# A hybrid decoder trunk on one core: where the second inverse root stands at a change of sub-layer

## The chip, the cores and the metric

One core of a Trainium2 chip runs the whole computation in one launch. The metric is the device time of a run in microseconds (us). The names of the engines are those of the profile: PE is TensorE, DVE is VectorE, ACT is ScalarE, POOL is GpSimd, and SP issues transfers.

## The reference

The input is a residual stream `x` of 512 tokens by 1024 channels in float32. Two layers follow one another, and each layer has four sub-layers. Each sub-layer reads `x` through an RMS norm, and its output goes through a second RMS norm before it is added to `x`:

```python
def rmsnorm(x, g):
    y = x * rsqrt(mean(x * x, axis=-1, keepdims=True) + EPS)
    return y * g

for i in range(DEPTH):                                    # DEPTH = 2
    h = rmsnorm(x, g_ffn1_pre[i])                         # 1: ffn1
    x = x + 0.5 * rmsnorm(swiglu(h, w1_gate[i], w1_up[i], w1_down[i]), g_ffn1_post[i])
    h = rmsnorm(x, g_mix_pre[i])                          # 2: mixer
    ... three head groups read h @ w_in[i]: stick-breaking attention, latent attention, gated convolution
    x = x + rmsnorm(concat(y_sb, y_mla, y_cv) @ w_out[i], g_mix_post[i])
    h = rmsnorm(x, g_ffn2_pre[i])                         # 3: ffn2
    x = x + 0.5 * rmsnorm(swiglu(h, w2_gate[i], w2_up[i], w2_down[i]), g_ffn2_post[i])
    h = rmsnorm(x, g_ple_pre[i])                          # 4: ple
    e = sigmoid(h @ w_ple_gate[i]) * (p[i] @ w_ple_proj[i])
    x = x + rmsnorm(e, g_ple_post[i])
```

So a change of sub-layer holds two norms back to back: the norm behind the old sub-layer, the addition to `x`, and the norm ahead of the new one. With two layers of four sub-layers there are seven such changes inside the kernel: ffn1 to mixer, mixer to ffn2, ffn2 to ple, ple to ffn1, and then the first three again in the second layer.

## The kernel before, in words

**Layout.** Channels lie on the 128 partitions and tokens along the free axis, so `x` is eight tiles of 128 by 512, the K slabs 0 to 7. Every float32 operand of a product is split into a rounded high part and a low rest (`xh`, `xl` for the activations, `wh`, `wl` for the weights), and a product of one slab is three matmuls: high by high, low by high, high by low. ACT makes the high part by a cast, DVE or POOL the low part by a subtraction.

**A change of sub-layer.** `finish` ends the old sub-layer. The last output tiles are computed for the first 256 tokens (`ca`) and then for the last 256 (`cb`), and each half has an inverse root of its own, `ra` and `rb_`. For a half, PE sums the squares with a column of ones into a PSUM tile `st` (L389), `Rstd.col` turns `st` into the inverse root `rt` by nine DVE operations on tiles of two columns (all of them L369: `r_v`, `r_y`, four that write `r_q`, `r_z`, `r_w`, `rt`), and `Rstd.row` lets PE transpose `rt` into a row (L402), which ACT copies to `rbs` (L403). Then `update(k, c)` scales `y` by `rbs` (L579, on DVE for the even slabs and on POOL for the odd ones) and adds it to `x` (L583 or L586, DVE).

`Entry` starts the new sub-layer. `half(c)` walks over the eight slabs: update of slab `k`, ACT's high part `xh` (L467), update of slab `k+1`, DVE's low part `xl` (L470), ACT's square of the new `x` (L434), and POOL's sum of the squares (L444). `products` lets PE follow the first half slab by slab for three output tiles (L488, L489 with `xh`; L493 with `xl`, one slab later). Behind slab 5 (`ROW_AT`) it calls `row_b`, so the two transposes of the row for the second half stand at that place in PE's order, and PE waits there until `rt` of the second half is made. Then comes `half(cb)` and the products of the second half (L286 to L288), a fourth output tile over all 512 tokens (`more`), and an inverse root over all four token blocks for the new sub-layer (`r.col`, on tiles of four columns), whose row (again L402) the new sub-layer's evacuations use.

**What sets the order.** Inside a `manual_schedule(engines={...})` block the named engine keeps the written order; everything else is placed by a scheduler when the kernel is built, and each engine then runs its list in order. In `half` DVE's order is the written one. Operations that were written outside of such a block can be placed between those inside it. Before the change `rb_.col()` stands outside, in `finish`, ahead of the construction of `Entry`.

Of the kernel before, what the change touches and what calls it, by code (L numbers as in the profile page):

```python
# [36 lines left out]
ROW_AT = 5  # L37
MORE = 1
LAG = 1
PROJ = 8  # L40
LAST_POOL = (2, 6)
DIRECT = 2
# [66 lines left out]
HALVES = (slice(0, S // 2), slice(S // 2, S))  # L109
# [49 lines left out]
def hybrid_trunk(ctx: ExitStack, tc: tile.TileContext, a: dict, out: bass.AP):  # L159
# [9 lines left out]
    def slot(dt=F32, name="s", tag="s"):  # L169
        return sp.tile([P, S], dt, tag=tag, name=name, bufs=SLOTS[tag])  # L170
# [6 lines left out]
    def bank(name="ps", tag=None):  # L177
        if tag is None:
            tag = dense[0][turn[0] % len(dense[0])]
            turn[0] += 1  # L180
        return ps.tile([P, S], F32, tag=tag, name=name, bufs=BANKS[tag])
# [10 lines left out]
    def f(ap):  # L192
        return ap.bitcast(F32)
# [45 lines left out]
    def gain(l, name, k):  # L239
        c = G_COLS[name] + k  # L240
        return gains[:, l, c:c + 1]
# [132 lines left out]
    class Rstd:  # L374
# [3 lines left out]
        def __init__(self, dim, cols=slice(0, S), tag="v", eps=None, keep=None):  # L378
            self.dim, self.blocks, self.st, self.tag = dim, blocks(cols), None, tag
            self.kw = dict(eps=eps if eps is None else eps[:, cols.start // P:cols.stop // P], keep=keep)  # L380
# [35 lines left out]
    def blocks(cols):  # L416
        return [slice(c, c + P) for c in range(cols.start, cols.stop, P)]
# [32 lines left out]
    class Entry:  # L450

        def __init__(self, l, name, update, row_b, tag):
            self.l, self.name, self.update, self.row_b = l, name, update, row_b
            self.xs = [(slot(F32R, "xh", tag), slot(F32R, "xl", tag)) for _ in range(NK)]
            self.tiles = [slot(name="sq") for _ in range(4)]
            self.sqs = [self.half(HALVES[0])]

        def half(self, c):  # L460
            sq = Squares(c, tiles=self.tiles)
            with tc.manual_schedule(engines={V.engine}):
                self.update(0, c)
                for k in range(NK):
                    g = gain(self.l, self.name, k)
                    h, lo = (t[:, c] for t in self.xs[k])
                    ia = A.activation(out=h, in_=x[k][:, c], func=AF.Copy, scale=g)  # L467
                    if k + 1 < NK:
                        self.update(k + 1, c)
                    iv = V.scalar_tensor_tensor(out=lo, in0=x[k][:, c], scalar=g, in1=f(h), op0=ALU.mult,  # L470
                                                op1=ALU.subtract)
                    sq.add(x[k][:, c])
            sq.fold()
            if c is HALVES[0]:
                self.tail = ia.ins, iv.ins
            return sq

        def products(self, tiles, more=lambda: None):
# [3 lines left out]
            with tc.manual_schedule(engines={T.engine}):  # L482

                for k in range(NK + LAG):
                    kw = dict(skip_group_check=True)
                    if k < NK:
                        for w, o in tiles:
                            T.matmul(o[:, ca], w[k][0], self.xs[k][0][:, ca], start=k == 0, stop=False, **kw)  # L488
                            T.matmul(o[:, ca], w[k][1], self.xs[k][0][:, ca], start=False, stop=False, **kw)  # L489
                    if k >= LAG:  # L490
                        j = k - LAG
                        for w, o in tiles:
# [28 lines left out]
    def finish(ys, sq, last, compute, evac, gcol, nxt, at, xtag="s", eps=None):  # L521
# [18 lines left out]
        ra, rb_ = Rstd(D, ca, eps=eps), Rstd(D, cb, eps=eps)  # L540
# [49 lines left out]
        if nxt is None:  # L590
# [17 lines left out]
                for k in order:  # L608
                    update(k, cb)
            return None  # L610
        rb_.col()
        return Entry(*nxt, update, row_b, xtag)


    def input_forms(l, name, xs, xtag):
# [116 lines left out]
    def ffn(l, idx, state, nxt, xtag="s", early=None):  # L732
# [121 lines left out]
        def evac(m, c, o):  # L854
            V.tensor_scalar(out=ys[m][:, c], in0=o[:, c], scalar1=half[:, l, idx, m:m + 1], scalar2=None, op0=ALU.mult)
            evac.square = o[:, c]

        return finish(ys, sq, last, compute, evac, None, nxt, AT_DOWN, eps=state.eps)

    def trig():  # L860
# [189 lines left out]
    def mixer(l, state, nxt):  # L1050
# [235 lines left out]
        def evac(m, c, o):  # L1286
            V.tensor_tensor(out=ys[m][:, c], in0=o[:, c], in1=ys[m][:, c], op=ALU.add)

        return finish(ys, sq, last, compute, evac, lambda k: gain(l, "mix_post", k), nxt, AT_OUT)

    def ple(l, state, nxt):
# [7 lines left out]
        def project(m):  # L1299
            if m % 4 == 0:  # L1300
                project.w = load_w(a["ple_proj"][l, m // 4], 8, P)
            o = bank()
            product(o, project.w[m % 4 * 2:m % 4 * 2 + 2], pin)
            t = aslot(name="pp")
            copy(E_PROJ, t, o)
            proj.append(t)

        def weights(m, on="vv"):
            return load_w(a["ple_gate"][l, m], NK, P, on)
# [8 lines left out]
        first = [(weights(m, ON_PLE.split()[m]), bank()) for m in range(FIRST)]  # L1318
        state.products(first, lambda: [project(m) for m in range(PROJ)])
        rb = state.row()  # L1320
        for m in range(PROJ, NK):
            project(m)
# [11 lines left out]
        def compute(m, c, tick=lambda: None):  # L1334
            o = bank()
            product(o, w[m], xs, cols=c, tick=tick)
            return o

        return finish(ys, sq, last, compute, evac, lambda k: gain(l, "ple_post", k), nxt, AT_PLE if nxt else AT_END, "m")

    cos = cst.tile([P, S], F32, name="cos")
# [65 lines left out]
```

## Time and profile before

| | |
|---|---|
| median of 3 runs | 2145.63 us (2145.09 to 2147.61) |
| the profiled execution's own time | 2147.86 us |
| its span in the trace | 2146.1 us |
| busy share: PE, DVE, ACT, POOL | 96%, 72%, 52%, 24% |
| mean granted TensorE clock | 0.984 |

The span runs from the first to the last instruction of the program in the trace, and the execution's own time is 1.8 us longer, for what lies around it. The busy shares are averages over stages: in the forty slices of the page PE stands at 90% or more nearly everywhere, and DVE moves between 30% and 90%. The columns of a timeline row are start, duration, engine, line, operation, output and inputs, and in brackets the idle time of the engine before it and what ended that time.

### The profile page before, as it was taken

How to read it: one execution, taken by the hardware profiler on the slowest of the kernel's cores; microseconds unless marked ns; L12 is line 12 of the kernel's file. 1: busy time of each engine (PE TensorE's matmuls, PEld its weight loads, DVE VectorE, ACT ScalarE, POOL GpSimd, SP SyncE). 2: the span in 40 equal slices, each digit the busy share in tenths (PEclk: the TensorE clock that was granted, in tenths of full speed). 3: DMA queues.
4: the chain of work that ended last, by engine and by line, in shares of the span. 5: the costliest groups of instructions: out<-in, count | busy, mean ns of one | idle time of the engine just before them, and what ended most of it. 6: DMA issues, size and time to landing. Idle time of an engine off the chain costs nothing.

```text
span 2146.1 us, 35942 instructions
## 1 busy us (share of the span) xinstructions
PE 2059.6 (96%) x13264; PEld 1874.2 (87%) x13264; DVE 1553.6 (72%) x2851; ACT 1116.6 (52%) x2296; POOL 506.6 (24%) x498
## 2 busy tenths in 40 slices
PE   8999999999989999999989999999999899999996
PEld 6999988887888999888879998888878889998886
DVE  7888754778878788636798786357788798885376
ACT  6556533555656555524565555235455565564243
POOL 3111012126432111003431110031263421100043
PEclk9999999999999999999999999999999999999998
DMA  7777332211133876332427763322111348753321
GB/s 218 172 180 177 89 104 72 91 60 52 55 79 108 196 173 148 100 99 79 122 84 196 178 163 93 98 68 93 53 59 46 88 126 192 180 137 96 98 73 65
DMA packets 139425, 244.73 MB, mean 114 GB/s; under 512 B 15600, under 2 KB 26096, under 8 KB 139248
## 3 DMA queue, kind: packets, MB, share of 16 engines
q1 hardware_dynamic: 117792, 204.00, 30.9%
q0 software_dynamic: 20736, 37.76, 11.2%
q8 instruction: 104, 1.70, 0.3%
q10 hardware_dynamic: 720, 0.67, 0.1%
q14 instruction: 73, 0.60, 0.1%
HBM read 240.27 MB, written 2.10 MB: 113 GB/s over the span
## 4 chain that ended last, share of the span: by engine, by line
PE 82%; DVE 12%; ACT 2%; issue 1%; DMA 1%; POOL 0%; SPq 0%; DVEq 0%; ACTq 0%; POOLq 0%
PE ps L286 9%; PE ps L287 9%; PE ps L288 9%; PE ux L698 6%; PE ux L697 6%; PE ux L696 6%; PE uy L698 3%; PE uy L697 3%; PE uy L696 3%; PE in L286 2%; PE in L287 2%; PE in L288 2%; DVE xl L470 2%; DVE wl L271 2%; PE uz L698 2%; PE uz L697 2%
## 5 line engine op out<-in xcount | busy, mean ns | idle before, releaser
L271 DVE TENSOR_TENSOR wl<-raw,wh 128x512 fp32r<-128x512 f32 (+2 forms) x893 | 605.8, 692 | 393.4 <-ACT wh L270 340.8
L270 ACT CAST wh<-raw 128x512 fp32r<-128x512 f32 (+1 forms) x934 | 548.7, 605 | 577.9 <-PE ps L287 275.1
L444 POOL TENSOR_TENSOR sq<-sq 128x256 f32<-128x256 f32 (+1 forms) x165 | 172.6, 1046 | 730.5 <-ACT sq L434 726.3
L287 PE MATMUL ps<-l,wh 128*128 128x512 f32 (+1 forms) x824 | 302.2, 367 | 0.0
L288 PE MATMUL ps<-h,wl 128*128 128x512 f32 (+1 forms) x824 | 301.8, 367 | 0.4 <-DVE wl L271 0.4
L286 PE MATMUL ps<-h,wh 128*128 128x512 f32 (+1 forms) x824 | 300.2, 368 | 0.0
L680 POOL DMA_DIRECT2D raw<-in_w_gu x144 | 125.9, 915 | 678.0 <-DMA raw<-in_w_gu 181.8
L698 PE MATMUL ux<-fh,wl 128*128 128x256 f32 x864 | 244.5, 283 | 0.0
L697 PE MATMUL ux<-fl,wh 128*128 128x256 f32 x864 | 244.5, 283 | 0.0
L696 PE MATMUL ux<-fh,wh 128*128 128x256 f32 x864 | 244.4, 283 | 0.0
L288 PEld LDWEIGHTS ps<-h,wl 128*128 128x128 f32 x824 | 155.4, 189 | 25.9 <-DVE wl L271 1.3
L287 PEld LDWEIGHTS ps<-l,wh 128*128 128x128 f32 x824 | 155.5, 189 | 24.8 <-DVE l L199 0.2
L286 PEld LDWEIGHTS ps<-h,wh 128*128 128x128 f32 x824 | 155.4, 189 | 24.6
L696 PEld LDWEIGHTS ux<-fh,wh 128*128 128x128 f32 x864 | 165.8, 192 | 0.5
L697 PEld LDWEIGHTS ux<-fl,wh 128*128 128x128 f32 x864 | 165.8, 192 | 0.5
L698 PEld LDWEIGHTS ux<-fh,wl 128*128 128x128 f32 x864 | 165.8, 192 | 0.0
L286 PE MATMUL ps<-xh,wh 128*128 128x512 f32 (+1 forms) x416 | 133.3, 356 | 15.5 <-ACT wh L270 9.8
L287 PE MATMUL ps<-xl,wh 128*128 128x512 f32 (+1 forms) x416 | 142.0, 352 | 1.2 <-DVE xl L470 1.2
L288 PE MATMUL ps<-xh,wl 128*128 128x512 f32 (+1 forms) x416 | 142.2, 350 | 0.0
L286 PEld LDWEIGHTS ps<-xh,wh 128*128 128x128 f32 x416 | 77.4, 196 | 28.7 <-ACT wh L270 11.2
L686 DVE TENSOR_TENSOR raw<-raw 128x512 f32<-128x512 f32 x144 | 98.6, 684 | 0.1
L287 PEld LDWEIGHTS ps<-xl,wh 128*128 128x128 f32 x416 | 80.6, 194 | 10.4 <-DVE xl L470 2.0
(347 smaller groups left out, 5237.1 us busy)
## 6 DMA issues: line engine op xcount, KB each, us to landing
raw<-in_w_gu SPq DMA_DIRECT2D x424, 256.0 KB, 4.0
raw<-in_w_down SPq DMA_DIRECT2D x160, 256.0 KB, 2.7
raw<-in_w_gu POOLq DMA_DIRECT2D x144, 256.0 KB, 5.1
raw<-in_win_f SPq DMA_DIRECT2D x60, 256.0 KB, 2.7
raw<-in_ple_gate SPq DMA_DIRECT2D x32, 256.0 KB, 2.7
raw<-in_wo_a SPq DMA_DIRECT2D x18, 256.0 KB, 2.8
raw<-in_w_down SPq DMA_DIRECT2D x32, 128.0 KB, 2.2
raw<-in_wo_b SPq DMA_DIRECT2D x12, 256.0 KB, 2.7
```

What stands on the lines that cost most here:

```text
L270: A.copy(out=h, in_=raw)
L271: (G if on == "g" else V).tensor_tensor(out=lo, in0=raw, in1=f(h), op=ALU.subtract)
L286: T.matmul(oc, wh, xh[:, cols], start=first and k == 0, stop=False, **kw)
L287: T.matmul(oc, wh, xl[:, cols], start=False, stop=False, **kw)
L288: product.last = T.matmul(oc, wl, xh[:, cols], start=False, stop=last and k == n - 1, **kw)
L444: G.tensor_tensor(out=self.acc[:, c], in0=self.acc[:, c], in1=self.last[:, c], op=ALU.add)
L470: iv = V.scalar_tensor_tensor(out=lo, in0=x[k][:, c], scalar=g, in1=f(h), op0=ALU.mult, op1=ALU.subtract)
L680: G.dma_start(out=self.raw[n], in_=self.part(m), accum_op=ALU.add)
L686: V.tensor_tensor(out=r, in0=r, in1=self.raw[p], op=ALU.add)
L696: T.matmul(o, wh, xh, start=first and k == 0, stop=False, **kw)
L697: T.matmul(o, wh, xl, start=False, stop=False, **kw)
L698: T.matmul(o, wl, xh, start=False, stop=k == 3, **kw)
```

## The change

`rb_.col`, the nine operations that make the second half's `rt`, is handed to `Entry` as a function, and `half` calls it in the first half's walk, directly behind the low part of slab 4 (the fifth slab). It now stands inside the block that keeps DVE's written order. What is computed is the same, and each operation is there as often as before.

```diff
 ROW_AT = 5
 MORE = 1
 LAG = 1
+COL_AT = 4
...
-        def __init__(self, l, name, update, row_b, tag):
-            self.l, self.name, self.update, self.row_b = l, name, update, row_b
+        def __init__(self, l, name, update, col_b, row_b, tag):
+            self.l, self.name, self.update, self.col_b, self.row_b = l, name, update, col_b, row_b
...
                     sq.add(x[k][:, c])
+                    if k == COL_AT and c is HALVES[0]:
+                        self.col_b()
...
-        rb_.col()
-        return Entry(*nxt, update, row_b, xtag)
+        return Entry(*nxt, update, rb_.col, row_b, xtag)
```

In the lists that follow `x_73` to `x_80` are the slabs 0 to 7 of `x`, and the kernel after counts its lines one to three higher.

DVE at the first change, ffn1 to mixer, before:

```order
L369 SCALAR_TENSOR_TENSOR r_v<-st,eps 128x2
L470 SCALAR_TENSOR_TENSOR xl<-x_77,gains,xh 128x256
L579 TENSOR_TENSOR y<-y,rbs 128x256
L369 TENSOR_SCALAR r_y_4198<-r_v 128x2
L586 TENSOR_TENSOR x_79<-y,x_79 128x256
L470 SCALAR_TENSOR_TENSOR xl<-x_78,gains,xh 128x256
L369 TENSOR_TENSOR r_q<-r_v,r_y_4198 128x2
L586 TENSOR_TENSOR x_80<-y,x_80 128x256
L369 TENSOR_TENSOR r_q<-r_q,r_y_4198 128x2
L470 SCALAR_TENSOR_TENSOR xl<-x_79,gains,xh 128x256
L369 SCALAR_TENSOR_TENSOR r_z<-r_q,r_y_4198 128x2
```

The same place after:

```order
L471 SCALAR_TENSOR_TENSOR xl<-x_77,gains,xh 128x256
L370 SCALAR_TENSOR_TENSOR r_v<-st,eps 128x2
L370 TENSOR_SCALAR r_y_4250<-r_v 128x2
L370 TENSOR_TENSOR r_q<-r_v,r_y_4250 128x2
L370 TENSOR_TENSOR r_q<-r_q,r_y_4250 128x2
L370 SCALAR_TENSOR_TENSOR r_z<-r_q,r_y_4250 128x2
L370 TENSOR_TENSOR r_q<-r_v,r_z 128x2
L370 TENSOR_TENSOR r_q<-r_q,r_z 128x2
L370 SCALAR_TENSOR_TENSOR r_w<-r_q 128x2
L370 SCALAR_TENSOR_TENSOR rt<-r_w,r_z 128x2
L582 TENSOR_TENSOR y<-y,rbs 128x256
L589 TENSOR_TENSOR x_79<-y,x_79 128x256
```

The nine operations stood singly or in pairs between the operations of slabs 4 to 7 and of the weights; now they follow one another, and the operations of slabs 5 to 7 stand behind them. Further down, the second half's first operations (`y`, `x_73`, `x_74`) have moved ahead of `xl` of slab 7 (`x_80`), and two subtractions for weights (`wl`) behind it.

DVE at the third change, ffn2 to ple, near the end of the second half, before:

```order
L586 TENSOR_TENSOR x_78<-y,x_78 128x256
L470 SCALAR_TENSOR_TENSOR xl<-x_77,gains,xh 128x256
L579 TENSOR_TENSOR y<-y,rbs 128x256
L586 TENSOR_TENSOR x_79<-y,x_79 128x256
L470 SCALAR_TENSOR_TENSOR xl<-x_78,gains,xh 128x256
L586 TENSOR_TENSOR x_80<-y,x_80 128x256
L470 SCALAR_TENSOR_TENSOR xl<-x_79,gains,xh 128x256
L271 TENSOR_TENSOR wl<-raw,wh 128x512
L470 SCALAR_TENSOR_TENSOR xl<-x_80,gains,xh 128x256
L271 TENSOR_TENSOR wl<-raw,wh 128x512 x5
```

The same place after:

```order
L272 TENSOR_TENSOR wl<-raw,wh 128x512
L471 SCALAR_TENSOR_TENSOR xl<-x_77,gains,xh 128x256
L582 TENSOR_TENSOR y<-y,rbs 128x256
L589 TENSOR_TENSOR x_79<-y,x_79 128x256
L471 SCALAR_TENSOR_TENSOR xl<-x_78,gains,xh 128x256
L589 TENSOR_TENSOR x_80<-y,x_80 128x256
L471 SCALAR_TENSOR_TENSOR xl<-x_79,gains,xh 128x256
L272 TENSOR_TENSOR wl<-raw,wh 128x512 x2
L471 SCALAR_TENSOR_TENSOR xl<-x_80,gains,xh 128x256
L272 TENSOR_TENSOR wl<-raw,wh 128x512 x2
```

More of the weights' subtractions stand ahead of the last slab's `xl`: from `r_v` to that point there are five, where there were three. At the two changes from ffn1 to mixer one subtraction of 128 by 288 has moved ahead of the last `xl` in the same way.

ACT at the third change, where the row for the second half is copied, before:

```order
L467 ACTIVATE xh<-x_79,gains 128x256
L434 ACTIVATE sq<-x_79 128x256
L185 COPY pp<-ps 128x512
L434 ACTIVATE sq<-x_80 128x256
L467 ACTIVATE xh<-x_80,gains 128x256
L403 COPY rbs<-rb 128x256
L467 ACTIVATE xh<-x_73,gains 128x256
```

The same place after:

```order
L186 COPY pp<-ps 128x512
L468 ACTIVATE xh<-x_79,gains 128x256
L435 ACTIVATE sq<-x_79 128x256
L468 ACTIVATE xh<-x_80,gains 128x256
L435 ACTIVATE sq<-x_80 128x256
L404 COPY rbs<-rb 128x256
L271 CAST wh<-raw 128x512
L186 COPY pp<-ps 128x512 x2
L468 ACTIVATE xh<-x_73,gains 128x256
```

Here the copy of the row still stands behind `xh` and the square of slab 7, as before. At the changes to the mixer and to the two ffn sub-layers it has moved ahead of `xh` of slab 6 (`x_79`).

## The prediction, made before the result was known

> **What bounds the kernel now.** I read the page first, then the waits of the row's transposes, then DVE's share in the stretches around them.
>
> ```profile
> PE 2059.6 (96%) x13264; PEld 1874.2 (87%) x13264; DVE 1553.6 (72%) x2851; ACT 1116.6 (52%) x2296; POOL 506.6 (24%) x498
> ```
>
> PE is the bound over the whole span: a microsecond saved on it counts only where PE waits. The view of the transposes' line says for whom they wait, and four of its rows in the timeline say how long.
>
> ```profile
>   DVE rt L369: 27.2, 10
> ...
> 378.08 0.43 PE L402 MATMUL rb<-ident,rt 128*128 128x128 f32 x2 [3.91 <-DVE rt L369]
> 1010.87 0.43 PE L402 MATMUL rb<-ident,rt 128*128 128x128 f32 x2 [1.93 <-DVE rt L369]
> 1083.49 0.69 PE L402 MATMUL rb<-ident,rt 128*128 128x128 f32 x2 [4.44 <-DVE rt L369]
> 1444.58 0.69 PE L402 MATMUL rb<-ident,rt 128*128 128x128 f32 x2 [2.93 <-DVE rt L369]
> ```
>
> Ten waits make 27.2 us, and seven of them are the second half's rows that this change is about; the four shown have a mean of 3.3 us. That is the prize. The windows (length, DVE busy, granted clock, DMA share, GB/s) say what the wait stands behind:
>
> ```profile
> 1003.00:1027.00 24.00, 23.03 (x47) 1.00 0.13 44
> 1438.00:1459.00 21.00, 20.13 (x42) 0.79 0.05 14
> sum 160.00, DVE 154.82; mean DVE 22.12
> ```
>
> The last row sums seven such windows, one at each change: DVE is busy for 97% of them. PE waits there for an engine that has no time to give. An earlier `rt` only changes what DVE does first; the second half of `x` comes no sooner unless DVE gets work off its list or loses less idle time.
>
> **What the nine operations cost, divided and undivided.** The first change, divided (DVE, with one row of POOL):
>
> ```profile
> 371.75 0.15 DVE L369 SCALAR_TENSOR_TENSOR r_v<-st,eps 128x2 f32<-128x2 f32 x1
> 371.82 0.47 DVE L470 SCALAR_TENSOR_TENSOR xl<-x,gains,xh 128x256 fp32r<-128x256 f32 x1
> ...
> 373.10 0.70 DVE L369 TENSOR_SCALAR r_y<-r_v 128x2 int32<-128x2 int32 x1
> 373.71 0.41 DVE L586 TENSOR_TENSOR x<-y,x 128x256 f32<-128x256 f32 x1
> ...
> 374.44 0.15 DVE L369 TENSOR_TENSOR r_q<-r_v,r_y 128x2 f32<-128x2 f32 x1
> 374.51 0.41 DVE L586 TENSOR_TENSOR x<-y,x 128x256 f32<-128x256 f32 x1
> ...
> 377.26 0.69 DVE L271 TENSOR_TENSOR wl<-raw,wh 128x512 fp32r<-128x512 f32 x1
> 377.87 0.15 DVE L369 SCALAR_TENSOR_TENSOR rt<-r_w,r_z 128x2 f32<-128x2 f32 x1
> 378.95 0.42 DVE L579 TENSOR_TENSOR y<-y,rbs 128x256 f32<-128x256 f32 x1 [0.33 <-ACT rbs L403]
> 372.15 1.62 POOL L444 TENSOR_TENSOR sq<-sq 128x256 f32<-128x256 f32 x2 [1.33 <-ACT sq L434]
> ```
>
> The distance of two starts is what an operation takes from DVE's list. `r_q` takes 0.07 us (374.44 to 374.51), because its neighbour does not need its result. `r_y` takes 0.61: POOL's sums run at that time, and I read the 0.54 above 0.07 as a wait for POOL. By all nine such distances the divided form takes 1.96 us of DVE here, of which about 1.2 are two waits for POOL. Undivided, the same nine stand elsewhere in this trace, first and last of them:
>
> ```profile
> 1062.81 0.16 DVE L369 TENSOR_SCALAR r_v<-st 128x2 f32<-128x2 f32 x1 [0.21 <-PE st L389]
> 1064.38 0.16 DVE L369 SCALAR_TENSOR_TENSOR rt<-r_w,r_z 128x2 f32<-128x2 f32 x1
> ```
>
> Eight steps take 1.57 us, 0.196 each, since each needs the one before; with 0.07 for the last, 1.64. Without POOL's waits, then, 0.77 becomes 1.64. POOL's operations stay and will hold up whatever DVE runs instead, except that such a wait can fill one of the chain's pauses. I take +0.8 us of DVE at each change. The lower bound is 1.64 - 1.96 = -0.3 (POOL holds up nothing in the chain, and nothing else in its place); the upper one is +1.9 (two more waits of 0.54). I take the value near the unblocked rows because DVE is full on both sides: a wait that leaves the chain falls on an update.
>
> [...]
>
> What DVE gets back is the idle time ahead of the second half's first `y`, as `rbs` will be there early:
>
> ```profile
> 646.75 0.42 DVE L579 TENSOR_TENSOR part<-part,rbs 128x256 f32<-128x256 f32 x1
> 1011.74 0.42 DVE L579 TENSOR_TENSOR y<-y,rbs 128x256 f32<-128x256 f32 x1 [0.54 <-ACT rbs L403]
> 1084.62 0.42 DVE L579 TENSOR_TENSOR pp<-pp,rbs 128x256 f32<-128x256 f32 x1 [1.19 <-ACT rbs L403]
> 1445.71 0.43 DVE L579 TENSOR_TENSOR y<-y,rbs 128x256 f32<-128x256 f32 x1 [0.59 <-ACT rbs L403]
> ```
>
> That is 0.33 at 379, nothing at 647 (two weight subtractions covered it), 1.19 at 1085, 0.59 at 1446. At 1012 the 0.54 stays, because ACT still copies the row behind `xh` of slab 7, which now comes after the chain. PE's own part needs no price: the transposes and their 0.05 us of reaction are the same, and they are only issued earlier. No transfer and no POOL operation is added; POOL's four scalings follow the row. In the written order DVE could now stand still for `st`, with all of slabs 5 to 7 queued behind; `r_v` started without idle time even ahead of slab 4's `xl` (371.75), so I price that at nothing.
>
> **What of this reaches the end of each change.** At a change to the mixer PE ends with the products of the last slab. The rows are the last `xl` on DVE, PE's first use of it, and the sums of squares behind the products:
>
> ```profile
> 391.51 0.47 DVE L470 SCALAR_TENSOR_TENSOR xl<-x,gains,xh 128x256 fp32r<-128x256 f32 x1
> 392.51 0.28 PE L287 MATMUL in<-xl,wh 128*128 128x256 f32 x1
> 396.46 0.39 PE L389 MATMUL st<-con,sq 128*128 128x1 f32 x3
> 1458.26 0.47 DVE L470 SCALAR_TENSOR_TENSOR xl<-x,gains,xh 128x256 fp32r<-128x256 f32 x1
> 1460.08 0.28 PE L287 MATMUL in<-xl,wh 128*128 128x256 f32 x1
> 1025.10 1.04 DVE L470 SCALAR_TENSOR_TENSOR xl<-x,gains,xh 128x256 fp32r<-128x256 f32 x1
> 1026.20 0.39 PE L287 MATMUL ps<-xl,wh 128*128 128x256 f32 x1 [0.19 <-DVE xl L470]
> ```
>
> First change (372 to 396). DVE: +0.8 - 0.33 + 0.4 for the 128 by 288 subtraction now ahead of the last `xl` (an estimate: a 256-wide `xl` takes 0.39, from 371.82 to DVE's next start) = +0.87. The last `xl` ended at 391.98 and PE took it at 392.51, 0.53 later; it will be 0.34 too late. PE has ten 256-wide and twelve 512-wide matmuls from there to 396.46, 3.95 us, so 0.116 for a 256-wide one; in the new order one of each kind less stands behind it, 0.35. **Change: 0.0.**
>
> Fifth change (1438 to 1460). DVE +0.8 - 0.59 + 0.4 = +0.6. PE took the last `xl` 1.35 us after its end, so 0.75 are left, with 0.35 for the order. **Gain: 1.0.**
>
> Third and seventh (ffn2 to ple). DVE +0.8, plus two more subtractions ahead of the last `xl`, 0.61 each (377.26 to 377.87): +2.0, and some 0.3 of slack at the weights' casts, so 1.7; PE was already waiting for it (0.19). For that six fewer 256-wide matmuls stand behind it, 0.7, and five 512-wide ones of the next tile now stand ahead, 1.15. **Gain: 0.1 each**, with filler products taking up the row's wait as before.
>
> At a change to an ffn the end is set by the row over all four blocks, whose `rt` stands at the end of DVE's list:
>
> ```profile
> 675.77 0.16 DVE L369 SCALAR_TENSOR_TENSOR rt<-r_w,r_z 128x4 f32<-128x4 f32 x1
> 677.06 0.38 PE L402 MATMUL rb<-ident,rt 128*128 128x128 f32 x2
> 1113.65 0.16 DVE L369 SCALAR_TENSOR_TENSOR rt<-r_w,r_z 128x4 f32<-128x4 f32 x1
> 1114.47 0.49 PE L402 MATMUL rb<-ident,rt 128*128 128x128 f32 x3
> 1744.00 0.16 DVE L369 SCALAR_TENSOR_TENSOR rt<-r_w,r_z 128x4 f32<-128x4 f32 x1
> 1744.31 0.40 PE L402 MATMUL rb<-ident,rt 128*128 128x128 f32 x2 [0.30 <-DVE rt L369]
> ```
>
> Second (677): `rt` was 1.13 us ahead of PE; 0.8 of it go to DVE's delay. **Gain: 0.3** at most. Sixth (1744): PE already waits for this `rt`, so DVE's delay is PE's. **Loss: 0.7.** Fourth (1114): DVE is 0.4 earlier (+0.8 - 1.19), and `rt` was 0.66 ahead. **Gain: 1.0.**
>
> The sum is 0.0 + 0.3 + 0.1 + 1.0 + 1.0 - 0.7 + 0.1 = 1.8 us. The profiled execution (2147.86, span 2146.1) would go to 2146.1; it lies 2.2 above the median, so I set the difference against the median: 2145.63 - 1.8 = **2143.8 us**. About 0.2%, 4.3 us, is what a measurement of this kernel tells from no change.
>
> **The rivals.** *PE keeps its head start.* PE's rows between 378 and 396 have no gap, which speaks for PE as the bound behind the row; then most of the row's wait is won. The wait of 3.3 us shrinks to the delay that slabs 6 and 7 of the first half now have behind the chain, 1.64 and some POOL, say 1.8: 1.5 us by seven is 10, time 2135. Against it stand the 97% of DVE. The granted clock belongs to this rival: it is 0.79 around the wait of 2.93 us and 1.00 around the one of 1.93, so shorter waits would also give PE back up to 0.21 of 21 us at such a change; where PE waits for DVE anyway, it gains nothing. [...]
>
> *The chain costs DVE nothing.* With -0.3 in place of +0.8, 1.1 us less per change, the first, second, sixth, third and seventh gain 1.1 each and the other two about 0.35, as PE's own work limits them: 1.8 + 5.5 + 0.7 = 8.0, time 2137.6. [...]
>
> *POOL holds up the chain* (the other side). With +1.9, the row at 1744 and the last slabs at 392, 1026 and its twin come 1.1 us later, the row at 677 loses 0.8, the rest loses its gain: the sum falls by about 7.5 to a loss of 5.7, time 2151. It is slower by over 0.2% once the chain takes some 1.8 us more than the divided form. For it speaks `r_y` above; against it that only two POOL sums stand near 372, and their waits are paid today too.
>
> *That nothing moves* is excluded: the lists differ at all seven changes.
>
> **How the numbers follow.** Forecast, DVE stays the bound and the gains are small: 0.54. PE's head start: 0.22. The chain for nothing: 0.12. POOL in the chain: 0.12. The likeliest gives 2143.8. The range runs from 2135.5 (just above the first rival, half of whose chance I leave out) to 2149.0 (the forecast with +1.5 for the chain, most of the third rival left out). Faster 0.35, same 0.52, slower 0.13; the forecast's own spread gives a little to both sides.
>
> **What would show it.** Right: the row's transposes wait 0 to 1.5 us instead of 1.9 to 4.4; nine L370 operations step by 0.2 us, with one or two of 0.6; DVE's idle ahead of `y` is gone except at the changes to ple; PE gets new waits, for `xh` of slab 6 and `xl` of slab 7 of the first half and for `xl` in the second; the row near 1744 waits longer. Wrong: PE without gaps through the second half and the sums of squares at 396 two microseconds earlier (PE's head start), or steps of 0.6 all along the chain (POOL).

## The result, and the profile after

Slower, by 0.56%: the changed kernel takes 2158.98 us (median of 5 runs, 2154.01 to 2162.6) against 2145.63 (median of 5 runs, 2145.09 to 2147.89). The ratio is 1.0056, 95% interval 1.0043 to 1.0070. The forecast was 2143.8 us, with a range that ended at 2149.0.

The profiled execution of the changed kernel took 2156.18 us (span 2154.4). Its line of busy times, and the rows' transposes that answer to those shown of before:

```profile
PE 2068.2 (96%) x13264; PEld 1876.0 (87%) x13264; DVE 1553.7 (72%) x2851; ACT 1115.6 (52%) x2296; POOL 503.6 (23%) x498
```
```profile
375.14 0.43 PE L403 MATMUL rb<-ident,rt 128*128 128x128 f32 x2 [0.60 <-DVE rt L370]
1009.46 0.27 PE L403 MATMUL rb<-ident,rt 128*128 128x128 f32 x1
1082.05 0.32 PE L403 MATMUL rb<-ident,rt 128*128 128x128 f32 x1 [0.65 <-DVE rt L370]
1443.66 0.32 PE L403 MATMUL rb<-ident,rt 128*128 128x128 f32 x1 [0.60 <-DVE rt L370]
```

The waits that the change is about are short now: 3.91, 1.93, 4.44 and 2.93 us have become 0.60, 0, 0.65 and 0.60. DVE's busy time is the same to 0.1 us. Where the time went is in the view that adds PE's waits up by what ended them (total, number, longest). Before:

```profile
PE rb L402 <- DVE rt L369: 27.2, 10, 4.4
...
PE in L488 <- ACT xh L467: 3.8, 3, 1.7
...
PE ps L488 <- ACT xh L467: 3.3, 4, 1.0
...
PE ps L493 <- DVE xl L470: 1.7, 2, 0.9
PE ps L287 <- DVE xl L470: 1.2, 4, 0.4
```

After:

```profile
PE rb L403 <- DVE rt L370: 9.5, 8, 3.7
...
PE ps L491 <- ACT xh L468: 7.3, 9, 1.0
PE ps L496 <- DVE xl L471: 6.2, 6, 2.0
PE in L491 <- ACT xh L468: 6.0, 6, 1.7
...
PE in L496 <- DVE xl L471: 4.5, 4, 2.0
PE ps L288 <- DVE xl L471: 4.0, 7, 0.9
...
PE in L288 <- DVE xl L471: 1.9, 2, 0.9
```

The wait for `rt` fell by 17.7 us. The waits for `xl` rose from 2.9 to 16.6 us and those for `xh` from 7.1 to 13.3: 19.9 us in all, in many shorter waits. The first change shows how. DVE after the change:

```profile
372.52 0.15 DVE L370 SCALAR_TENSOR_TENSOR r_v<-st,eps 128x2 f32<-128x2 f32 x1
372.70 0.58 DVE L370 TENSOR_SCALAR r_y<-r_v 128x2 int32<-128x2 int32 x1
...
374.92 0.16 DVE L370 SCALAR_TENSOR_TENSOR rt<-r_w,r_z 128x2 f32<-128x2 f32 x1
375.00 0.42 DVE L582 TENSOR_TENSOR y<-y,rbs 128x256 f32<-128x256 f32 x1
...
375.79 0.48 DVE L471 SCALAR_TENSOR_TENSOR xl<-x,gains,xh 128x256 fp32r<-128x256 f32 x1
376.19 0.95 DVE L589 TENSOR_TENSOR x<-y,x 128x256 f32<-128x256 f32 x1
377.06 0.96 DVE L582 TENSOR_TENSOR y<-y,rbs 128x256 f32<-128x256 f32 x1
377.94 0.96 DVE L471 SCALAR_TENSOR_TENSOR xl<-x,gains,xh 128x256 fp32r<-128x256 f32 x1
378.83 1.81 DVE L589 TENSOR_TENSOR x<-y,x 128x256 f32<-128x256 f32 x2
380.57 0.94 DVE L471 SCALAR_TENSOR_TENSOR xl<-x,gains,xh 128x256 fp32r<-128x256 f32 x1
381.43 1.82 DVE L272 TENSOR_TENSOR wl<-raw,wh 128x512 fp32r<-128x512 f32 x2
383.18 0.47 DVE L471 SCALAR_TENSOR_TENSOR xl<-x,gains,xh 128x256 fp32r<-128x256 f32 x1
```

The four scalings of the second half on POOL, before, and after with the two sums of squares (`sq`) that follow them (two views of two kernels):

```profile
379.00 3.60 POOL L579 TENSOR_TENSOR y<-y,rbs 128x256 f32<-128x256 f32 x4 [2.21 <-ACT rbs L403]
```
```profile
376.05 3.44 POOL L582 TENSOR_TENSOR y<-y,rbs 128x256 f32<-128x256 f32 x4 [1.97 <-ACT rbs L404]
379.46 1.77 POOL L445 TENSOR_TENSOR sq<-sq 128x256 f32<-128x256 f32 x2
```

They start when the row is there. After the change that is 3 us earlier, and from 376.19 up to the end of slab 7's `xl` (381.51) every 256-wide DVE operation takes about 0.95 us instead of 0.41 to 0.48. The `xl` of slab 6 (377.94) lies beside the scalings, that of slab 7 (380.57) beside the sums, which POOL makes only when the scalings are done. PE waits for both:

```profile
376.47 0.39 PE L491 MATMUL in<-xh,wh 128*128 128x256 f32 x1 [0.90 <-ACT xh L468]
376.69 0.28 PE L492 MATMUL in<-xh,wl 128*128 128x256 f32 x1
...
378.44 0.28 PE L492 MATMUL in<-xh,wl 128*128 128x256 f32 x1
378.96 0.62 PE L496 MATMUL in<-xl,wh 128*128 128x256 f32 x3 [0.25 <-DVE xl L471]
381.56 0.62 PE L496 MATMUL in<-xl,wh 128*128 128x256 f32 x3 [1.98 <-DVE xl L471]
...
383.70 0.58 PE L288 MATMUL in<-xl,wh 128*128 128x256 f32 x1 [0.93 <-DVE xl L471]
```

Before, PE had slabs 6 and 7 still to do when the row came at 378.08, and they covered the time in which POOL's scalings slowed the start of the second half (PE did them at half the clock, from 378.59 to 382.00). The second half's first `xl` on DVE and PE's first use of it, before:

```profile
381.05 0.95 DVE L470 SCALAR_TENSOR_TENSOR xl<-x,gains,xh 128x256 fp32r<-128x256 f32 x1
```
```profile
382.95 0.28 PE L287 MATMUL in<-xl,wh 128*128 128x256 f32 x1
```

That `xl` is slow too, but it ends at 382.00, 0.95 us before PE comes to it. After, PE has done part of that work early and stands without cover. Its last wait ends at 383.70, and from there it is PE that sets the pace: it runs without a wait up to the sums of squares, at 398.84 instead of 396.46.

### The profile page after: what moved, and what is told of

Same layout as the page of the kernel before. It is cut to its first block, busy times and chain, and to the rows that moved or that the text cites. A ratio compares the mean times of both kernels' runs of the same rounds, so it can differ in the third digit from the quotient of the medians.

```text
span 2154.4 us, 35929 instructions
## 1 busy us (share of the span) xinstructions
PE 2068.2 (96%) x13264; PEld 1876.0 (87%) x13264; DVE 1553.7 (72%) x2851; ACT 1115.6 (52%) x2296; POOL 503.6 (23%) x498
## 4 chain that ended last, share of the span: by engine, by line
PE 82%; DVE 13%; ACT 3%; issue 1%; DMA 1%; POOL 0%; SPq 0%; DVEq 0%; ACTq 0%; POOLq 0%
PE ps L288 10%; PE ps L287 10%; PE ps L289 10%; PE ux L700 6%; PE ux L699 6%; PE ux L698 6%; PE uy L700 3%; PE uy L698 3%; PE uy L699 3%; PE in L288 2%; PE in L289 2%; PE in L287 2%; DVE wl L272 2%; DVE xl L471 2%; PE uz L698 2%; PE uz L699 2%
## 5 line engine op out<-in xcount | busy, mean ns | idle before, releaser
L287 PE MATMUL ps<-xh,wh 128*128 128x512 f32 (+1 forms) x416 | 138.9, 363 | 12.3 <-ACT wh L271 8.9
```

The source lines that it names most:

```text
L287: T.matmul(oc, wh, xh[:, cols], start=first and k == 0, stop=False, **kw)
```

## The experiments

The numbers used below: the time by the ratio to the kernel before, run beside it on the same chip; and the **shift**, read from the start of the rows' transposes in a kernel's trace less that in the first trace of before. A change's own shift is what it adds between the row ahead of it and a row behind it. With m for the mixers' changes (1, 5), f for those to an ffn (2, 4, 6), p for ple (3, 7), the first trace after has m +2.0, +1.1; f -1.3, -0.5, +1.3; p +2.2, +2.2. They sum to 7.0 of the 8.3 us between the two spans; the rest lies elsewhere. The m values end at the second row inside the mixer (447 and 1515), the f values at the next row behind the ffn, the p values at 1066 and 2101. A half-clock window (one of 3.41 us in which PE gets half its clock, shown in the last section) that falls here or there is worth up to 1.7 us in one shift.

**Where the chain stands (e1).** `COL_AT = 4` becomes `COL_AT = 7`.

> The undivided chain stands behind the low part of slab 7 of the first half instead of slab 4 (nothing of the second half can pass the first half's last slabs, and the weights' subtractions lie where the scheduler puts them). Order theory (the loss of 13 us comes from what an early rt lets in ahead of xl of slab 7 and of the second half's xl of slab 0): the loss is gone, 2144 to 2149. Chain theory (nine dependent operations in one block cost DVE and PE about 2 us at each change, wherever they stand): 2154 to 2162. Clock theory (many short waits in place of one let the granted clock fall in the second half): one wait of 4 to 5 us again, time 2146 to 2150.

Measured: 2159.33 us, ratio 1.0057 (1.0043 to 1.0072). The order theory falls as I put it: with nothing of the second half ahead of any `xl` of the first, the loss is the same. The time lies in the range of the chain theory. But it is another loss than that of the change. PE's waits for `rt` are 35.3 us here against 27.2 before and 9.5 after: the undivided chain, with nothing beside it, is simply late. The place that the change chose is better for the row and worse for what follows.

**What stands ahead of the last `xl` (e2, e3, e4).** In `half`, for the second half (e2 and e4):

```diff
+                with ExitStack() as e:
+                    if c is HALVES[1]:
+                        e.enter_context(tc.issue_after(self.tail[1]))
-                self.update(0, c)
+                    self.update(0, c)
```

and for the fourth tile's weights (e3 and e4):

```diff
+                    if k == 1 and c is HALVES[1]:
+                        self.tail = ia.ins, iv.ins
```

> As the changed kernel, but DVE's first operation of the second half is held until xl of slab 7 of the first half; three second-half operations (y and two x, 2.85 us by the trace, most of it waits for POOL) leave the place ahead of it. Order theory: PE's wait for that xl falls from 1.98 us to below 0.5 at the first change; the wait for the second half's first xl stays or grows to 1.5 to 2.5, since two weight subtractions still stand ahead of it: 2150 to 2157. Chain theory: no change, 2157 to 2161. Clock theory: fewer waits, but one of them still about 2 us, 2152 to 2158.

> As the changed kernel, but the subtractions for the fourth tile's weights may come only behind xl of slab 1 of the second half (at the three changes to the mixer or to an ffn that have them and where they stood ahead of xl of slab 0). Order theory: the wait of 1.98 us stays, the one of 0.93 for the second half's first xl is gone: 2152 to 2157. Chain theory: no change, 2157 to 2161. Clock theory: one wait less per change, but the clock still falls behind the 1.98: 2154 to 2160.

> Both edits at once: the second half held behind xl of slab 7 of the first, and the fourth tile's weights behind xl of slab 1 of the second. Order theory: the whole loss is taken back and the early row is won, 2138 to 2147. Chain theory: 2156 to 2161. Clock theory: waits at the changes sum to about 2 us instead of 4 to 6, so 2140 to 2148 as well; the traces must then tell whether the slow PE steps (46 us in the trace before, 55 in the one after) or the waits moved.

Measured: e2 2153.77 us, 1.0036 (1.0024 to 1.0048); e3 2164.89, 1.0087; e4 2165.91, 1.0086. Holding the half takes back about a third. It does not remove the wait: at the first change 2.79 us are left, now for `xh` of the second half's first slab, and POOL's scalings still lie on the `xl` of slabs 6 and 7. Late weights look like a loss of 6 us more, but that is not made at the changes: between the rows at 447 and 474, inside the mixer, both kernels lose several us (e3 7.2, e4 4.7), because the scheduler placed the mixer's own list in another order. These two times say nothing about the question; at the changes themselves e4 has m -0.5, -1.0 and f -1.7, -1.5, +0.6.

**Which changes lose (e5, e6, e14, e15).** The chain is handed over only where the name allows it:

```diff
+        col_b = rb_.col
+        if nxt[1] not in EARLY_COL:      # e5: ple; e6: all but ple; e14: the ffns; e15: the mixer
+            rb_.col()
+            col_b = lambda: None
-        return Entry(*nxt, update, rb_.col, row_b, xtag)
+        return Entry(*nxt, update, col_b, row_b, xtag)
```

> The undivided chain only at the two changes to ple; the other five as before. Supply theory (at a change to ple the three last xl come later, and ten more 512-wide products stand ahead of the row that the new sub-layer's outputs wait for: 2.2 us later at each of the two in the trace after, nothing of it regained): +4 to +5, 2150 to 2152. Theory that the loss is made at the five other changes, by waits in place of one wait: within 2 us of before.

> The undivided chain only at the five changes to the mixer and to an ffn; the two to ple as before. If the loss is the sum of both kinds: 2151 to 2155, and the two sub-kernels' differences add up to the 13 us of the whole change, with 2 to 3 us for where the half-clock windows happen to fall. If ple alone loses: 2145 to 2148.

> The change as it is, but only at the three changes to an ffn. POOL theory, by the shifts in the trace after (-1.3, -0.5, +1.3): 2144 to 2148 and slower than the run with the scalings on DVE by 3 to 5 us. If the loss of the five changes (9 to 10 us by the run without ple) is spread over ffn and mixer changes alike: 2149 to 2152.

> The change as it is, but only at the two changes to the mixer. By the shifts in the trace after (+2.0, +1.1): 2148 to 2150. If the mixers carry the loss that the ffn changes do not show: 2151 to 2155. The three partial kernels (ple, ffn, mixer) should add up to the whole change's 13 us.

Measured: ple alone 1.0018 (1.0009 to 1.0027), all but ple 1.0041 (1.0027 to 1.0055), the ffns 1.0009 (0.9998 to 1.0019), the mixers 1.0025 (1.0014 to 1.0035). The parts add up: 0.18 + 0.09 + 0.25 = 0.52%, against 0.56. The mixers carry nearly half of the loss at two changes, ple a third at its two, and the ffns at most little.

**The clock (e7).** In the kernel before, 20 matmuls that nobody reads ahead of the row, at five changes:

```diff
+            if fill:
+                for _ in range(20):
+                    T.matmul(rb, *fill, start=True, stop=True, skip_group_check=True)
             for b in range(n):
                 T.transpose(...)
```

> The kernel before, with 20 matmuls of 256 columns whose result nobody reads (2.4 us at the full clock, written to the row's bank ahead of the row) in the wait for rt at the five changes to the mixer and to an ffn. Clock theory (a window of 3.41 us in which PE idles for more than half brings half the clock in the next one, up to 1.7 us each): nothing is later, since the waits are 2.9 to 4.4 us long, and five to eight of the fifteen slow windows go: 2134 to 2141. Theory that the clock is no matter of the waits: 2145 to 2148.

Measured: 2150.7 us, 1.0017 (1.0006 to 1.0028). Slower, so the expectation of the clock theory failed. In the trace only one of the eight half-clock windows around the five waits is left, yet the stretches up to the rows of the new sub-layer get shorter by only 0.1 to 1.4 us each, 3.8 in all: the half-clock windows of before lay mostly where PE had time to spare. Elsewhere this trace has windows that the first trace of before lacks, at 449, 517 and 1756. Over all its runs the granted clock is higher than that of before, 0.989 against 0.986; why its median is higher by 5 us all the same stays open.

**A mixture (e8).** The edits of e2 at the five changes and of e3 at the ffns, ple as before:

```diff
-                    if c is HALVES[1]:
+                    if c is HALVES[1] and self.name != "ple_pre":
...
-                    if k == 1 and c is HALVES[1]:
+                    if k == 1 and c is HALVES[1] and self.name.startswith("ffn"):
```

> The undivided chain at five changes (ple as before), the second half held behind the first half's last xl at all five, and the fourth tile's weights behind the second half's slab 1 at the changes to an ffn only. By the shifts of the rows in the traces of the earlier runs (held: +1.3 and -0.9 at the mixers; held and late: -1.7, -1.5 and +0.6 at the ffns): -2.3, so 2142 to 2147. If the changes do not add up: 2148 to 2154.

Measured: 2148.31 us, 1.0015 (1.0006 to 1.0024). Most of the loss of the five changes (0.41% in e6) is gone, nothing is won. Its own trace has -2.0 at the five changes, as forecast, but the time does not follow it.

**POOL (e9 to e12).** e9 is e2 with POOL's scalings of the second half behind the first half's last sum of squares; the other three put the second half's odd scalings on DVE (e10 in the changed kernel, e11 in the kernel before, e12 in e2):

```diff
+                if c is HALVES[1]:                       # e9
+                    pool.enter_context(tc.issue_after(self.sqs[0].sum.ins))
...
-            e = G if k % 2 or nxt is None and k in LAST_POOL else V
+            e = G if k % 2 and (c is ca or nxt is None) or nxt is None and k in LAST_POOL else V
```

> As the kernel with the second half held behind the first half's last xl, and POOL's four scalings of the second half also held, behind POOL's last sum of squares of the first half. POOL theory (the early row sets POOL's scalings going some 4 us earlier, and each DVE operation beside them takes 0.95 us instead of 0.41, among them the xl of slabs 5 to 7 that PE waits for): PE's wait for xl of slab 7, 2.79 us at the first change in the held kernel, falls to 1 or below; the scalings then lie on the second half's first operations, as in the kernel before: 2146 to 2151. Theory that DVE's order alone matters: as the held kernel, 2152 to 2156.

> The changed kernel with the second half's four odd scalings on DVE instead of POOL at every change. POOL theory: no operation of 0.95 us on DVE behind the early row; xl of slab 7 ends some 3 us earlier than in the changed kernel, the second half's first xl too, and 4 times 0.41 us more work on DVE is less than the 2.2 us that the scalings cost it: 2140 to 2150. Order theory (what stands ahead of xl matters, not how long POOL makes it): 2156 to 2162, since one more scaling stands ahead of xl of slab 7. Clock theory: little change, 2153 to 2160.

> Control: the kernel before with the same four scalings on DVE. There POOL's scalings lie on y, x and the first xl of the second half behind the wait for the row. POOL theory: DVE gains 2.2 - 1.6 = about 0.5 us per change, PE mostly has slack there: 2142 to 2146. Otherwise, with 1.6 us more on DVE at each change: 2147 to 2153.

> The changed kernel with the second half held behind the first half's last xl and the four scalings on DVE: the early row without POOL on top of it and without second-half work ahead of the last xl. POOL theory: the best of the four, 2136 to 2146. Chain theory (the undivided chain by itself costs DVE 0.8 to 1.6 us at each change): 2148 to 2156.

Measured: e9 2157.28 us, 1.0048 (1.0032 to 1.0064); e10 2156.8, 1.0045 (1.0028 to 1.0062); e11 2162.95, 1.0070 (1.0054 to 1.0086); e12 2157.01, 1.0048 (1.0031 to 1.0066). As times, the POOL theory failed. (The 2.79 us that the text for e9 ascribes to `xl` of slab 7 are the wait for `xh` named above.) The traces tell two things apart. e10, e11 and e12 lose 4.7 to 7.7 us in each mixer, between the same rows as e3 and e4 and for the same reason. At the changes they gain. DVE at the first change of e10:

```profile
374.10 0.16 DVE L370 SCALAR_TENSOR_TENSOR rt<-r_w,r_z 128x2 f32<-128x2 f32 x1
...
375.37 0.42 DVE L589 TENSOR_TENSOR x<-y,x 128x256 f32<-128x256 f32 x1
375.70 0.42 DVE L582 TENSOR_TENSOR y<-y,rbs 128x256 f32<-128x256 f32 x1
376.04 1.03 DVE L471 SCALAR_TENSOR_TENSOR xl<-x,gains,xh 128x256 fp32r<-128x256 f32 x1
376.99 0.96 DVE L589 TENSOR_TENSOR x<-y,x 128x256 f32<-128x256 f32 x1
377.87 0.41 DVE L582 TENSOR_TENSOR y<-y,rbs 128x256 f32<-128x256 f32 x1
378.21 0.47 DVE L471 SCALAR_TENSOR_TENSOR xl<-x,gains,xh 128x256 fp32r<-128x256 f32 x1
```

and POOL and PE there:

```profile
376.05 1.61 POOL L445 TENSOR_TENSOR sq<-sq 128x256 f32<-128x256 f32 x2 [2.79 <-ACT sq L435]
```
```profile
378.73 0.63 PE L496 MATMUL in<-xl,wh 128*128 128x256 f32 x3 [0.66 <-DVE xl L471]
380.67 0.39 PE L288 MATMUL in<-xl,wh 128*128 128x256 f32 x1 [0.72 <-DVE xl L471]
```

Two operations of about 1 us are left, beside POOL's two sums. From the end of `rt` to the end of slab 7's `xl` it is 378.68 - 374.26 = 4.4 us; in the changed kernel 381.51 - 375.08 = 6.4, with eight operations between the two in both. Over the five changes to a mixer or an ffn the shifts sum to:

| shift of five changes, us | scalings on POOL | all on DVE |
|---|---|---|
| chain as before | 0 (e17: -0.2) | -2.1 (e11) |
| early chain | +2.6, +2.9 (after, e18) | -6.8 (e10) |
| early chain, second half held | +0.9 (e2) | -7.0 (e12) |

In these traces the early chain loses 2.6 us with the scalings on POOL and wins 4.7 without them. Such a sum is rough: e5, whose five changes are as before, has -3.5, and e6, with the five changes as in after, +6.1. The two differences between the columns in the lower rows, 9.4 and 7.9, are more than twice as large as e5's. Holding POOL back (e9, +4.4) does not help: its scalings then run from 377.17 on and lie on the second half's first operations, where PE has no work left to cover them.

**The same without the mixer's other order (e13, e16).** e13 has the early chain at the ffns only, held, scalings on DVE there; e16 adds the mixers, held, with the scalings of slabs 1 and 3 on DVE, a set that leaves the mixer's list as it was:

```diff
+            if nxt and c is cb and k in ON_DVE.get(nxt[1], ()):   # e13: 1, 3, 5, 7 for the ffns
+                e = V                                             # e16: also 1, 3 for the mixer
```

> The undivided chain only at the three changes to an ffn, with the second half held behind the first half's last xl and its four odd scalings on DVE there; the mixers' own lists stay as in the kernel before. POOL theory, by the shifts of these three changes in the runs with everything on DVE (-2.2, -1.5, -0.1): 2140 to 2144, faster than the kernel before. Theory that the undivided chain itself costs DVE too much: 2147 to 2152.

> As the first kernel of this set, and at the two changes to the mixer the undivided chain too, with the second half held and the scalings of slabs 1 and 3 on DVE (with slab 5 as well the mixer's own lists would be placed in another order). POOL theory: two scalings still run beside xl of slabs 5 to 7, half of the loss at the mixers is taken back, 0 to +0.7 each: 2140 to 2145. Chain theory: 2150 to 2155.

Measured: e13 2145.37 us, 0.9996 (0.9985 to 1.0007); e16 2143.69, 0.9994 (0.9981 to 1.0006). e13 misses the range of the POOL theory, e16 lies in it. At the mixers the change cost 0.25% (e15); with the half held and two scalings off POOL the five changes together cost nothing. At the ffns 0.09% becomes -0.04%, which is within the intervals. So the loss at the five changes (e6, 0.41%) goes with the scalings and the place of the second half taken together. Which carries more is not settled: by the times, e8 has most of the loss back with all scalings on POOL (0.15% left); by the table, e10 has all of it back without holding anything. Neither kernel is measurably faster than the one before. Their profiled executions had spans of 2139.3 and 2140.5 us, 6 us below that of before, their medians 0.6 above and 1.1 below it: single traces differ from medians by several us.

**Each kernel once more (e17, e18).**

> The kernel before, profiled a second time. If the half-clock windows lie on a grid of their own that each launch meets at another phase, their places change (in the first trace 15 of them up to 2100 us, none between 390 and 640), while idle time (76.1 us, all gaps over 60 ns) and the remainder (span less idle less half of the busy time in slow windows, 2045.8 us) stay within 2 us each. If windows belong to places in the program, they fall where they did.

> The changed kernel, profiled a second time. If each wait costs PE about 0.26 us beyond the idle time shown (0.16 at its last step, 0.10 at its first), the remainder again lies 6 to 9 us above that of the kernel before (2053.6 against 2045.8 in the first pair) at about the same idle time, and the rest of the difference in time is in the slow windows. If the remainder of the first pair was chance, it lies within 3 us.

I split each span into idle time (gaps over 60 ns on PE), slow clock (half of PE's busy time in the windows at half clock), and the remainder:

| us | span | idle | slow clock | remainder |
|---|---|---|---|---|
| before, two traces | 2146.1, 2145.5 | 76.1, 77.0 | 24.2, 21.2 | 2045.8, 2047.4 |
| after, two traces | 2154.4, 2153.5 | 75.8, 70.3 | 25.0, 33.7 | 2053.6, 2049.5 |

Both expectations came true only in part. Of before's 15 windows 13 came back at the same place, so two launches do not show that the grid's phase is free. The remainder of after lies 5.0 us above before in the mean, 2.1 to 7.8 by pairs. Taken as means, the 8.2 us of the traces are idle -3.5, slow clock +6.7, remainder +5.0. The remainder has a likely source in the rows shown above. The matmul at 378.44 occupies 0.52 us up to the next start: 0.12 is the distance of two starts ahead of it (378.32 to 378.44), 0.25 the idle time shown, and 0.16 is what its row (0.28) lasts beyond the 0.12 (the profile models the ends of matmuls, so the 0.16 is no measurement of its own); and the first one behind a wait (376.47) takes 0.22 to the next start instead of 0.12. By these rows I estimate that a wait costs PE some 0.26 us more than the idle time shown (0.16 and 0.10). After has 77 and 71 gaps over 0.15 us, before 58 in both traces: 16 more by 0.26 are 4.2 us. All traces bear this out in the main: over the nineteen other than e7's the remainder grows by 0.32 us with each gap more (correlation 0.91).

**The clock over all runs.** The slow clock of two traces spreads too far to judge by, but the span and the granted clock of every run are known (the clock to 0.001, which is 2.1 us of one run). Span times (1 - clock) is what the half clock took of a run at most, since PE also idles in such windows:

| means over runs | span, us | clock | taken by the half clock, us | rest, us |
|---|---|---|---|---|
| before (35 runs) | 2143.5 | 0.9861 | 29.8 | 2113.7 |
| after (5) | 2156.5 | 0.9832 | 36.2 | 2120.3 |
| ple alone, e5 (12) | 2148.4 | 0.9858 | 30.4 | 2118.0 |
| all but ple, e6 (6) | 2153.0 | 0.9817 | 39.5 | 2113.5 |
| the ffns, e14 (12) | 2145.7 | 0.9832 | 35.9 | 2109.7 |
| the mixers, e15 (12) | 2149.4 | 0.9841 | 34.2 | 2115.2 |
| five held, two on DVE, e16 (12) | 2142.6 | 0.9867 | 28.6 | 2114.0 |

By this measure about half of the whole change's 13.0 us is half-clock time (+6.4). At the five changes it accounts for all of the loss (e6: +9.7 of 9.5), at ple for next to nothing (+0.6 of 4.9), and in e16 it is gone. That fits the first change: PE idles in short waits, and the window behind them, from 383.60 on, runs at half the clock where PE sets the pace. That it goes like this at each change and in each run is not shown.

## Why the prediction was wrong

**What held.** DVE is full at the changes (after, it is busy for 156.2 of 160 us in the same seven windows; its busy time holds what POOL costs it, as the rows of 0.95 us show). The chain costs about what was said: at the first change 2.48 us of DVE's list, steps of 0.196 us and two of 0.6 by POOL, against 1.96 divided; that is +0.5, where +0.8 was taken. The waits of the row's transposes are 0 to 1.07 us, and the new waits stand where they were expected: `xh` of slab 6, `xl` of slab 7, `xl` of the second half.

**The first step that failed is the pricing of POOL.** "POOL's operations stay and will hold up whatever DVE runs instead" counted what POOL takes from DVE in all, not on what it falls. The text even said that "POOL's four scalings follow the row", and drew nothing from it. They start 3 us earlier and make an operation take 0.95 in place of 0.41, about 0.54 more, for four operations 2.2 us, and they push POOL's two sums behind them, at the place where PE waits for the last two `xl` of the first half. DVE's total does not change (1553.6 and 1553.7 us), and so a sum over DVE's list could not see it. The rows show the collision; as times, only e16 shows it, and there together with the held half.

**At a change to the mixer the end was put at the wrong operation.** This is the second step that failed. The working asked when the last `xl` comes: 393.60 instead of 391.98. That was not far from the forecast (+1.3 with the 0.36 that the trace was late ahead of the change, against +0.87). But PE has been the bound since its wait for the second half's *first* `xl`. That wait is what should have been followed; it ends at 383.70, and the next window has half the clock. Forecast 0.0 and a gain of 1.0; measured by the shifts a loss of 2.0 and 1.1, by the partial kernel 5.4 us for the two (0.25% of 2144.74), of which at most 4.4 are half-clock time.

**At the changes to ple work ahead of the row was counted as gained.** This is the third. At the third change the sums of squares are 1.67 us later (1.1 without the 0.58 that the trace was late ahead of it), and more 512-wide products stand between them and the row for which the new sub-layer's outputs wait: 37 instead of 31, and from the row at 992 on 78 instead of 67. The last sums ahead of these products, and the row, before:

```profile
1027.74 0.73 PE L389 MATMUL st<-con,sq 128*128 128x1 f32 x6
...
1035.44 0.27 PE L402 MATMUL rb<-ident,rt 128*128 128x128 f32 x1
```

After:

```profile
1029.41 0.50 PE L390 MATMUL st<-con,sq 128*128 128x1 f32 x4
...
1038.29 0.38 PE L403 MATMUL rb<-ident,rt 128*128 128x128 f32 x2
```

7.7 us have become 8.9. Eleven products of 0.23 us are 2.5 us, and the row is 2.3 us later than the trace was at 992. The prediction took 1.15 us of such products as work done; the rest of ple waits for the row, not for PE, and nothing is regained by 1066 (+2.7 us). Forecast a gain of 0.1 each, measured a loss of 2.3 and of 2.4 in the trace of ple alone, and 0.18% (3.9 us) as its time.

**At the changes to an ffn** the agreement is luck. Forecast were gains of 0.3, 1.0 and -0.7 at the row over all four blocks; there all three come later in the first trace, by 1.4, 0.2 and 2.2 us. The slack of `rt` was taken as PE's gain, and PE came later, not earlier. The row near 1744 does not wait for `rt`, though that was forecast: `rt` ends at 1747.20, the row starts at 1748.81 behind products. Part of the loss comes back inside the ffn, where PE now waits less for DVE's `g`. Before and after, behind the second change:

```profile
685.24 0.47 PE L286 MATMUL ps<-xh,wh 128*128 128x512 f32 x1 [2.12 <-DVE g L751]
```
```profile
687.43 0.47 PE L287 MATMUL ps<-xh,wh 128*128 128x512 f32 x1 [0.97 <-DVE g L753]
```

Behind the wait of 2.12 us the trace of before has a half-clock window (685.79 to 689.20), after has none. At the next row behind the ffns the gains are 1.3, 0.5 and -1.3, which is 0.5 in all where 0.6 was forecast; the partial kernel shows no measurable effect.

**The rivals.** "POOL holds up the chain" had the right engine and side, and the wrong place: POOL holds up what stands *behind* the chain. It was given 0.12 and 2151 us. "PE keeps its head start" needed a cover that is not there, and it had shorter waits give PE clock back; over the runs the granted clock fell from 0.986 to 0.983. No rival priced the number of waits.

What is not settled: the traces of the two kernels differ by 8.2 us, the medians by 13.3. The rest is in executions that were not traced; of those only the span and the clock are known. Nor is it settled how the loss at the five changes divides between the scalings and the place of the second half.

## What to carry to other kernels

Before an event is moved earlier, list everything that starts on it, on all engines; an operation that is off the path where it stands can land on the path. Where the operations of one engine take longer beside another's (0.95 us instead of 0.41 here), price the other engine by the place of the collision, not by a total. And follow the last wait of the engine that is the bound: removing one long wait buys nothing if the work that it stood ahead of was the cover for the next.

## What the runs showed of the hardware

**The granted clock came in windows of 3.41 us, full (1.00) or half (0.50).** Two windows of before and two of after at the first change (length, then PE, PEld, DVE, ACT, POOL busy, granted clock, DMA share, GB/s):

```profile
375.17:378.59 3.42, 0.51 (x5) 0.51 (x5) 3.35 (x9) 1.67 (x5) 1.54 (x2) 1.00 0.00 0
378.59:382.00 3.41, 3.41 (x19) 3.41 (x18) 3.05 (x6) 1.96 (x5) 3.00 (x4) 0.50 0.35 91
```
```profile
380.18:383.60 3.42, 1.21 (x7) 0.90 (x7) 3.42 (x6) 1.26 (x4) 2.11 (x3) 1.00 0.13 28
383.60:387.01 3.41, 3.31 (x12) 3.08 (x13) 3.34 (x8) 1.55 (x4) 1.50 (x2) 0.50 0.21 58
```

Here the window behind one in which PE was busy for 0.51 or 1.21 us of 3.41 has half the clock. Over the twenty traces of this case (up to 2100 us), 147 of 162 windows at full clock with PE idle for half of it or more were followed by one at half clock, 20 of 53 with 45 to 50%, and 27 of 505 with 20 to 45%; of some 11200 with less, 37 were, which idle time does not explain. The idle time of the second view (2.21 us) comes from two waits, of 1.98 and 0.93 us, and not from a single gap.

**DVE beside POOL.** In the changed kernel's rows at the first change (376.19 to 381.51) a 256-wide two-input operation on DVE took about 0.95 us beside a POOL scaling or sum of squares of the same width, and 0.41 to 0.48 without. What in the hardware holds DVE up is not shown. By these rows the four scalings on POOL cost DVE more there (about 2.2 us, an estimate: 4 by 0.54) than doing them itself would (4 by 0.41 = 1.6).

**A wait cost PE more than its idle time**, some 0.26 us at the full clock, an estimate from the changed kernel's rows at 376.47 and 378.44; over nineteen traces the remainder grew by 0.32 us with each gap more. By either figure several short waits cost more here than one of the same sum.
